# Gate and up of a SwiGLU layer as 2x2 block products in seven multiplications, on normed token halves

## The chip, the cores and the metric

The kernel runs on one core of a Trainium2 chip. Its time is the device time of one execution in microseconds (us). The engines are TensorE (PE, with its weight loads as PEld), VectorE (DVE), ScalarE (ACT), GpSimd (POOL) and SyncE (SP), whose queue issues nearly all DMAs here.

## The reference, cut to what matters

One step of a decoder layer for 1024 prompt tokens and 8 sampled tokens, 1032 rows in all, with 1024 channels. Two mixers come first (sparse attention and a gated delta rule); the change doesn't touch them. Then:

```python
x = x + jnp.sum(gates * proj, axis=2) @ w_out          # w_out [1024, 1024]
hn = rms_norm(x, norm_ffn)
gg, uu = jnp.split(hn @ w_gate_up, 2, axis=-1)         # w_gate_up [1024, 2 * 2816]
x = x + (jax.nn.silu(gg) * uu) @ w_down                # w_down [2816, 1024]
```

All of it is in float32.

## The kernel before, in words

Every large product is done on transposed data: the stationary operand is a 128x128 block of weights, the moving operand is the activations, channels on the partitions and tokens along the free axis, in three chunks of 344 tokens (`CW`, `NCH`). To keep float32 precision each operand is split exactly into a high and a low part of type float32r (`split`, L186: the high part is a copy on ACT, L187; the low part a subtraction on DVE, L188), and `mm3` (L158) forms each product from three matmuls, high-high (L163), high-low (L164) and low-high (L165). A weight slice of 128 columns comes through `split_w` (L132): one DMA to `wraw`, split to `whi` and `wlo`, two buffers of each.

The end of the kernel is `w45`. After the merge of the two mixers (`yhi`, `ylo`) comes `w_out` (L1544): for each of 8 slices and 3 chunks, 24 matmuls to a PSUM tile `pj`; its eviction adds the residual to `x2` in SBUF (L1548), squares it, splits the square, multiplies x by the gain (L1554), splits that into `hhi` and `hlo`, and lets two more matmuls with a matrix of ones add the squares of the slice to `acc` (L1557). The mean square of a token is complete only after the last slice; `rs`, its reciprocal root, is then formed on DVE (L1570 to L1576). It is not needed by the products of the feed-forward layer: `mlp` (L1585) multiplies the unnormed `hhi`, `hlo` by the weights and applies `rs` when a PSUM tile is evicted (L1604).

`mlp` has four groups of 6, 6, 5 and 5 of the 22 slices of the hidden dimension. For each slice: gate and up weights, 3 chunks of 2 x 24 matmuls, then SiLU, product and split into `act`, which stays in SBUF. After a group, its part of the down projection is added to `x2` (L1614); the last group also stores the result (`store_y`).

Order: the kernel is written as a program of tile operations, and a scheduler sets the order on each engine's queue from priorities and modelled times; at run time every engine works its queue in that order, and semaphores hold it where an operand or a buffer isn't ready. The same holds for SP's queue of DMAs.

## Time and profile before

| | us |
|---|---|
| median of 3 runs | 1839.82 |
| lowest, highest | 1836.02, 1849.74 |
| span of the profiled execution | 1845.2 |
| PE busy in it | 1797.4 (97%) |
| DVE busy, ACT busy | 1084.1 (59%), 781.3 (42%) |
| `w_out` (from 982.6 to 1083.5) | 100.9 |
| feed-forward layer to the end (from 1083.5) | 761.7 |

The profiled execution has no time of its own beside its span; that span is 5.4 us above the median of the runs. Engine times are busy times of one core. A matmul is listed with its whole duration, and matmuls overlap in the array, so the time that one takes of a stream is read from the distance of two starts, not from its duration.

### The profile page before, as it was taken

What the parts mean: (1) busy time and instruction counts of PE and PEld (TensorE: products, weight loads), DVE (VectorE), ACT (ScalarE), POOL (GpSimd) and SP (SyncE); (2) the same over time, 40 slices, a digit from 0 to 9 for tenths busy, and PEclk for the clock granted to TensorE, in tenths of its full rate; (3) what the DMA queues carried; (4) which work ended last, traced back from release to release, by engine and by line L of the source; (5) the groups of instructions that cost most, each with busy time, mean ns of one, the idle gap of its engine ahead of it and who ended that gap; (6) DMA issues with size and microseconds to landing.
All of it is one profiled execution on the core that took longest, in us unless ns stands there. A gap on an engine that the chain in (4) does not pass through costs nothing.

```text
span 1845.2 us, 29553 instructions
## 1 busy us (share of the span) xinstructions
PE 1797.4 (97%) x11532; PEld 1721.5 (93%) x11532; DVE 1084.1 (59%) x2576; ACT 781.3 (42%) x1470; POOL 42.8 (2%) x68
## 2 busy tenths in 40 slices
PE   5998999998999999999999999999999999999998
PEld 5997989998998898878799999999999999999998
DVE  7766568998898767787566573333333233333332
ACT  4567378778644345677344432211221112212222
POOL 3001100000000000000000000000000000000000
PEclk9999999999999989999999999999999999999999
DMA  6115534435456433344665111111111121021122
GB/s 190 42 37 149 158 95 120 138 114 159 109 137 180 135 108 106 133 139 161 221 204 158 38 36 50 50 44 52 48 53 38 46 58 46 29 64 35 51 62 84
DMA packets 266063, 178.82 MB, mean 97 GB/s; under 512 B 37628, under 2 KB 251456, under 8 KB 264892
## 3 DMA queue, kind: packets, MB, share of 16 engines
q1 hardware_dynamic: 264196, 166.45, 30.5%
q0 software_dynamic: 1728, 10.49, 1.6%
q8 instruction: 91, 1.49, 0.3%
q14 instruction: 48, 0.39, 0.1%
HBM read 130.98 MB, written 46.02 MB: 96 GB/s over the span
## 4 chain that ended last, share of the span: by engine, by line
PE 88%; DVE 4%; DMA 4%; ACT 2%; issue 1%; SPq 0%; DVEq 0%; ACTq 0%
PE pj L163 24%; PE pj L165 24%; PE pj L164 24%; PE PT L1054 1%; PE PT L1022 1%; PE tq L1388 1%; PE PT L1023 1%; PE PV L1058 1%; PE PV L1059 1%; PE tq L1346 1%; DMA x<-d_G 1%; DMA x<-in_x_prompt 1%; PE tp L591 1%; PE ac L410 1%; PE ac L411 1%
## 5 line engine op out<-in xcount | busy, mean ns | idle before, releaser
L163 PE MATMUL pj<-hhi,whi 128*128 128x344 f32 x1056 | 337.4, 320 | 0.1
L164 PE MATMUL pj<-hlo,whi 128*128 128x344 f32 x1056 | 336.5, 319 | 0.0
L165 PE MATMUL pj<-hhi,wlo 128*128 128x344 f32 x1056 | 334.0, 320 | 0.0
L163 PE MATMUL pj<-xhi,whi 128*128 128x344 f32 x912 | 299.1, 328 | 6.0 <-ACT gs L860 5.0
L165 PE MATMUL pj<-xhi,wlo 128*128 128x344 f32 x912 | 295.9, 324 | 0.0
L164 PE MATMUL pj<-xlo,whi 128*128 128x344 f32 x912 | 294.8, 323 | 0.0
L187 ACT ACTIVATE whi<-wraw 128x1024 fp32r<-128x1024 f32 (+2 forms) x134 | 133.3, 995 | 331.5 <-PE pj L164 328.2
L1604 DVE TENSOR_TENSOR gu<-pj,rs 128x344 f32<-128x344 f32 x132 | 68.2, 517 | 263.5 <-PE pj L165 261.4
L163 PEld LDWEIGHTS pj<-hhi,whi 128*128 128x128 f32 x1056 | 198.5, 188 | 0.4 <-DVE gu L1604 0.4
L164 PEld LDWEIGHTS pj<-hlo,whi 128*128 128x128 f32 x1056 | 198.1, 188 | 0.0
L165 PEld LDWEIGHTS pj<-hhi,wlo 128*128 128x128 f32 x1056 | 197.8, 188 | 0.0
L188 DVE TENSOR_TENSOR wlo<-wraw,whi 128x1024 fp32r<-128x1024 f32 (+2 forms) x134 | 153.1, 1142 | 50.8 <-ACT whi L187 49.3
L163 PEld LDWEIGHTS pj<-xhi,whi 128*128 128x128 f32 x912 | 173.3, 190 | 10.0 <-ACT gs L860 6.5
L164 PEld LDWEIGHTS pj<-xlo,whi 128*128 128x128 f32 x912 | 173.1, 190 | 2.0 <-issue 1.1
L165 PEld LDWEIGHTS pj<-xhi,wlo 128*128 128x128 f32 x912 | 173.1, 190 | 1.5
L164 PE MATMUL pj<-act,whi 128*128 128x344 f32 x528 | 170.2, 322 | 0.0
L163 PE MATMUL pj<-act,whi 128*128 128x344 f32 x528 | 169.7, 321 | 0.0
L165 PE MATMUL pj<-act,wlo 128*128 128x344 f32 x528 | 167.8, 319 | 0.0
L1614 DVE TENSOR_TENSOR x<-pj,x 128x344 f32<-128x344 f32 x96 | 49.6, 517 | 169.0 <-PE pj L165 169.0
L187 ACT ACTIVATE act<-gu 128x344 fp32r<-128x344 f32 x66 | 32.5, 493 | 200.4 <-DVE gu L1606 200.4
L766 DVE TENSOR_SCALAR_CACHE_REDUCE kvb<-S,cand 128x384 bf16<-128x384 f32 (+3 forms) x128 | 103.7, 810 | 2.0
L163 PEld LDWEIGHTS pj<-act,whi 128*128 128x128 f32 x528 | 99.4, 188 | 0.5
(493 smaller groups left out, 3374.2 us busy)
## 6 DMA issues: line engine op xcount, KB each, us to landing
wraw<-in_w_gate_up SPq DMA_DIRECT2D x44, 512.0 KB
wraw<-in_w_in SPq DMA_DIRECT2D x38, 512.0 KB
d_g<-gs SPq DMA_DIRECT2D x48, 172.0 KB
wraw<-in_w_branch SPq DMA_DIRECT2D x12, 512.0 KB
wraw<-in_w_down SPq DMA_DIRECT2D x16, 384.0 KB
wraw<-in_w_down SPq DMA_DIRECT2D x16, 320.0 KB
gt<-d_g SPq DMA_DIRECT2D x8, 516.0 KB
d_y<-gt SPq DMA_DIRECT2D x8, 516.0 KB
```

The lines of the kernel that those rows point to most:

```text
L163: nc.tensor.matmul(ps, lh, rh, start=(j == 0), stop=False)
L164: nc.tensor.matmul(ps, lh, rl, start=False, stop=False)
L165: nc.tensor.matmul(ps, ll, rh, start=False, stop=(j == last))
L187: self.nc.scalar.activation(hi, src, AF.Copy)
L188: self.nc.vector.tensor_tensor(lo, src, hi.bitcast(F32), op=ALU.subtract)
L410: nc.tensor.matmul(p, lhs, self.ik2[:, 0, c0:c1], start=True, stop=False)
L411: nc.tensor.matmul(p, lhs, self.ik2[:, 1, c0:c1], start=False, stop=True)
L591: nc.tensor.transpose(p[:, j, :], c[:, 128 * n:128 * n + 128], self.ident)
L766: nc.vector.tensor_scalar(junk[:r, :n], s, thr[:r, j:j + 1], 0.0, op0=ALU.is_lt, op1=ALU.add, accum_out=cnt[:r, j:j + 1])
L1022: nc.tensor.matmul(p, q2[:, j, :], self.k2[:, g, 0, a:b], start=True, stop=False)
L1604: nc.vector.tensor_tensor(s[:, e], p, rs[:, t], op=ALU.mult)
L1614: nc.vector.tensor_tensor(x2(m)[:, t], p, x2(m)[:, t], op=ALU.add)
```

## The change

The output projection and the norm are done for two halves of 516 tokens, one after the other; the normed x is written in place in `x2`, and the residual before the norm goes to DRAM (`d_x2`) to be read again before the down projection. Gate and up of one slice are seen as a 2x2 block matrix A: gate and up are its rows, the first and second 512 input channels its columns. The normed half is a 2x2 block matrix B: channel halves by two quarters of 258 tokens. The product of the two comes from seven block products, with S0 to S3 (sums and differences of blocks of A, on DVE, per slice) and T1 to T4 (differences of blocks of B, once per half). Partial products accumulate in four PSUM tags A, B, D, F with two buffers each. The first three slices (`EARLY`) are computed on half 0 in the plain way, and with seven products on half 1 alone. The hidden activations of all 22 slices go to DRAM (`d_act`), and the down projection (`down`) starts when the last slice is done and reads them back, three `araw` buffers at a time. Comments and docstrings are removed as well, which shifts the line numbers: `split` keeps L187 and L188. The removed lines stand in the section on the kernel before; the diff below leaves them out, but for a few.

```diff
-FIRST, REST = (0, 1), (2,)
+HALF, QT, EARLY = 516, 258, 3
...
+        self.d_x2 = dp.tile([8, 128, T], F32, name="d_x2")
+        self.d_act = dp.tile([22, 128, T], F32, name="d_act")
...
-        self.pj_bufs, self.tp_bufs, self.ac_bufs = 3, 2, 2
+        self.pj_bufs, self.tp_bufs = 5, 2
-        self.acc = [self.pacc() for c in range(2)]
...
     def w45(self):
...
+        H = [None, None]
+        for s in range(2):
+            self.w_out(s, (yhi, ylo), x2)
+            self.ffn_norm(s, gf, x2)
+            if s == 0:
+                H[0] = self.half_blocks(0, h0, ("B11", "B21", "B12", "B22"))
         end_y()
+        h1, end_h1 = self.pool("h1")
+        ex, end_ex = self.pool("gx")
         self.end_pf()
         self.end_ps()
+        self.ps, end_ps = self.pool("psg", space=PSUM)
+        for f in range(EARLY):
+            self.gate_up_plain(f, H[0], ex)
+        H[1] = self.half_blocks(1, h1, ("B21", "B11"))
+        H[1].update(self.half_mixes(1, h1, H[1]))
+        H[0].update(self.half_mixes(0, h0, H[0]))
+        for f in range(EARLY):
+            self.gate_up(f, (1,), H, ex)
+        for f in range(EARLY, 22):
+            self.gate_up(f, (0, 1), H, ex)
+        end_ps()
+        end_ex()
+        end_h1()
+        end_h0()
+        self.down(x2)
         end_x()
 
+    def w_out(self, s, y, x2):
+        nc, I = self.nc, self.I
+        ts = slice(HALF * s, HALF * s + HALF)
+        sq, self.sqa = self.stage[:, 0:HALF], self.stage[:, HALF * (1 + s):HALF * (2 + s)]
+        for m in range(8):
+            xv = x2(m)
+            def evac(p, t0, t1):
+                nc.vector.scalar_tensor_tensor(xv[:, t0:t1], p, 0.5, xv[:, t0:t1], op0=ALU.mult, op1=ALU.add)
+            self.proj_T(self.wcols(I['w_out'][0], 128 * m), y, evac, HALF * s, HALF * s + HALF)
+            nc.scalar.activation(sq if m else self.sqa, xv[:, ts], AF.Square)
+            if m:
+                nc.vector.tensor_tensor(self.sqa, self.sqa, sq, op=ALU.add)
+            nc.sync.dma_start(self.d_x2[m, :, ts], xv[:, ts])
+    def ffn_norm(self, s, gf, x2):
+        nc = self.nc
+        n = 86
+        p = self.pproj()
+        for j in range(6):
+            nc.tensor.matmul(p[:n, j:j + 1], self.sqa[:, n * j:n * j + n], self.ones[:, 0:1], start=True, stop=True)
+        v, r, t = (self.nrm.tile([128, 6], F32, name=x, tag=x, bufs=1)[:n] for x in ("nv", "nr", "nt"))
+        nc.vector.tensor_scalar(v, p[:n, 0:6], 1.0 / 1024, EPS, op0=ALU.mult, op1=ALU.add)
+        self.rsqrt(r, v, t=t)
+        for c in range(2):
+            p = self.pproj()
+            for j in range(3):
+                i = 3 * c + j
+                nc.tensor.matmul(p[:, n * j:n * j + n], r[:, i:i + 1].to_broadcast([n, 128]), self.ident[:n, :n],
+                                 start=True, stop=True)
+            nc.scalar.activation(self.sqa[:, QT * c:QT * c + QT], p[:, 0:QT], AF.Copy)
+        for m in range(8):
+            xv = x2(m)[:, HALF * s:HALF * s + HALF]
+            nc.vector.scalar_tensor_tensor(xv, xv, gf[:, m:m + 1], self.sqa, op0=ALU.mult, op1=ALU.mult)
+    def quarter(self, s, name):
+        i, j = int(name[1]) - 1, int(name[2]) - 1
+        t0 = HALF * s + QT * j
+        return self.x2h[i][:, :, t0:t0 + QT]
+    def block(self, pool, src):
+        t = pool.tile([128, 2, 4, QT], F32R, name="hb", tag="hb", bufs=7)
+        self.split(t[:, 0], t[:, 1], src)
+        return t
+    def half_blocks(self, s, pool, names):
+        return {x: self.block(pool, self.quarter(s, x)) for x in names}
+    def half_mixes(self, s, pool, H):
+        nc = self.nc
+        B11, B12, B21, B22 = (self.quarter(s, x) for x in ("B11", "B12", "B21", "B22"))
+        out = {}
+        def sub(name, dst, a, b):
+            nc.vector.tensor_tensor(dst, a, b, op=ALU.subtract)
+            out[name] = self.block(pool, dst)
+        if "B22" not in H:
+            out["B22"] = self.block(pool, B22)
+        sub("T1", B11, B12, B11)
+        sub("T3", B12, B22, B12)
+        sub("T2", B22, B22, B11)
+        sub("T4", B21, B21, B22)
+        return out
+    def gate_up_plain(self, f, H, ex):
+        nc, gu = self.nc, self.I['w_gate_up'][0]
+        sg = ex.tile([128, HALF], F32, name="sg", tag="sg", bufs=2)
+        ws = [self.wcols(gu, 128 * f), self.wcols(gu, 2816 + 128 * f)]
+        for e, (wh, wl) in enumerate(ws):
+            for c in range(2):
+                tag = "ABDF"[2 * e + c]
+                p = self.ps.tile([128, 512], F32, name=tag, tag=tag, bufs=2)[:, :QT]
+                x1, x2 = H[f"B1{c + 1}"], H[f"B2{c + 1}"]
+                self.mm3(p, [(wh[:, k], wl[:, k], x[:, 0, k % 4], x[:, 1, k % 4])
+                             for k in range(8) for x in ((x1, x2)[k // 4],)])
+                v = sg[:, QT * c:QT * c + QT]
+                if e == 0:
+                    nc.scalar.activation(v, p, AF.Silu)
+                else:
+                    nc.vector.tensor_tensor(v, v, p, op=ALU.mult)
+        nc.sync.dma_start(self.d_act[f, :, 0:HALF], sg)
+    def gate_up(self, f, halves, H, ex):
+        nc, gu = self.nc, self.I['w_gate_up'][0]
+        view = lambda c0: gu.rearrange("(k p) n -> p k n", p=128)[:, :, c0:c0 + 128]
+        rg, ru = (self.wp.tile([128, 8, 128], F32, name="wraw", tag="wraw", bufs=self.raw_bufs) for _ in range(2))
+        nc.sync.dma_start(rg, view(128 * f))
+        nc.sync.dma_start(ru, view(2816 + 128 * f))
+        A11, A12, A21, A22 = rg[:, 0:4], rg[:, 4:8], ru[:, 0:4], ru[:, 4:8]
+        S = [self.stage[:, 512 * j:512 * j + 512].rearrange("p (k c) -> p k c", k=4) for j in range(4)]
+        sub = lambda d, a, b: nc.vector.tensor_tensor(d, a, b, op=ALU.subtract)
+        def operand(src):
+            self.op_n = (self.op_n + 1) % 7
+            tag = ("whi", "wlo", "wx", "whi", "wlo", "wx", "wx")[self.op_n]
+            pool, bufs = (ex, 3) if tag == "wx" else (self.wp, 2)
+            t = pool.tile([128, 8, 128], F32R, name=tag, tag=tag, bufs=bufs)
+            self.split(t[:, 0:4], t[:, 4:8], src)
+            return t
+        U = {}
+        st = self.x2h[f // 2 % 2][:, 2 * (f % 2):2 * (f % 2) + 2]
+        ps = {(t, s): self.ps.tile([128, 512], F32, name=t, tag=t, bufs=2)[:, :QT] for s in halves for t in "ABDF"}
+        def product(src, x, t, first):
+            a = operand(src)
+            for s in halves:
+                b, p = H[s][x], ps[t, s]
+                for k in range(4):
+                    lh, ll, rh, rl = a[:, k], a[:, 4 + k], b[:, 0, k], b[:, 1, k]
+                    nc.tensor.matmul(p, lh, rh, start=(first and k == 0), stop=False, skip_group_check=True)
+                    nc.tensor.matmul(p, lh, rl, start=False, stop=False, skip_group_check=True)
+                    nc.tensor.matmul(p, ll, rh, start=False, stop=(k == 3), skip_group_check=True)
+        def add(e, s, c, a, b):
+            nc.vector.tensor_tensor(st[:, e, HALF * s + QT * c:HALF * s + QT * c + QT], a, b, op=ALU.add)
+        def part(tag, p=None):
+            t = ex.tile([128, QT], F32, name=tag, tag=tag, bufs=2)
+            if p is not None:
+                nc.scalar.activation(t, p, AF.Copy)
+            return t
+        product(A12, "B21", "B", True)
+        product(A11, "B11", "A", True)
+        for s in halves:
+            add(0, s, 0, part("E", ps["A", s]), ps["B", s])
+        nc.vector.tensor_tensor(S[0], A21, A22, op=ALU.add)
+        product(S[0], "T1", "D", True)
+        sub(S[1], A11, A21)
+        product(S[1], "T3", "F", True)
+        sub(S[2], S[0], A11)
+        product(S[2], "T2", "A", False)
+        for s in halves:
+            U[s] = part("U", ps["A", s])
+            e = part("E")
+            nc.vector.tensor_tensor(e, U[s], ps["D", s], op=ALU.add)
+            add(1, s, 1, e, ps["F", s])
+        sub(S[3], A12, S[2])
+        product(S[3], "B22", "D", False)
+        for s in halves:
+            add(0, s, 1, U[s], ps["D", s])
+        product(A22, "T4", "F", False)
+        for s in halves:
+            t = slice(HALF * s, HALF * s + HALF)
+            add(1, s, 0, U[s], ps["F", s])
+            nc.scalar.activation(st[:, 0, t], st[:, 0, t], AF.Silu)
+            nc.vector.tensor_tensor(st[:, 0, t], st[:, 0, t], st[:, 1, t], op=ALU.mult)
+            nc.sync.dma_start(self.d_act[f, :, t], st[:, 0, t])
+    op_n = -1
+    def down(self, x2):
+        nc, dn = self.nc, self.I['w_down'][0]
+        self.pf, self.end_pf = self.pool("psd", space=PSUM)
+        self.pj_bufs = 4
+        self.open_psum("ps6")
+        ac, end_ac = self.pool("act", side="right")
         wk, end_wk = self.pool("mlp")
+        for m in range(8):
+            nc.sync.dma_start(x2(m), self.d_x2[m])
         groups = [(0, 6), (6, 12), (12, 17), (17, 22)]
         for gi, (f0, f1) in enumerate(groups):
+            act = []
             for f in range(f0, f1):
+                a = ac.tile([128, 2, T], F32R, name="act", tag="act", bufs=10)
+                raw = wk.tile([128, T], F32, name="araw", tag="araw", bufs=3)
+                nc.sync.dma_start(raw, self.d_act[f])
+                self.split(a[:, 0], a[:, 1], raw)
+                act.append((a[:, 0], a[:, 1]))
             for m in range(8):
+                def evac(p, t0, t1):
+                    xv = x2(m)[:, t0:t1]
+                    nc.vector.tensor_tensor(xv, p, xv, op=ALU.add)
+                self.proj_T(self.wcols(dn[128 * f0:128 * f1], 128 * m, f1 - f0), act, evac)
                 if gi == len(groups) - 1:
                     self.store_y(m, x2, wk)
         end_wk()
         end_ac()
+        self.end_ps()
+        self.end_pf()
 
...
```

How the order on the queues changes, at three places.

**PE, end of the output projection.** Before: the products of the next stage (`hhi`) stand right behind those of `w_out` (`yhi`), and the sums of squares (`ac`, L1557) among them.

```order
L163 MATMUL pj<-yhi,whi 128x344
L164 MATMUL pj<-ylo,whi 128x344
L165 MATMUL pj<-yhi,wlo 128x344
L163 MATMUL pj<-hhi,whi 128x344
L164 MATMUL pj<-hlo,whi 128x344
L165 MATMUL pj<-hhi,wlo 128x344
...
L1557 MATMUL ac<-sqh,onesr 128x344
```

Now, at the end of half 0 (`rs` in the first row is the sum of squares, `nr` the reciprocal roots; the rows with `whi_11333` are the last slice of half 0, those with `whi_11445` the first of half 1):

```order
L164 MATMUL pj_11364<-ylo_10251,whi_11333 128x258
L165 MATMUL pj_11364<-yhi_10250,wlo_11334 128x258
L1589 MATMUL pj_11393<-ones_1543,rs_10113 86x1 x6
L1597 MATMUL pj_11414<-ident_84,nr_11401 128x86 x3
L1597 MATMUL pj_11419<-ident_84,nr_11401 128x86 x3
L163 MATMUL pj_11450<-yhi_10250,whi_11445 128x258
L164 MATMUL pj_11450<-ylo_10251,whi_11445 128x258
```

The twelve small matmuls of the norm stand between two streams with nothing else between them; at the end of half 1 it is the same, with the first plain gate slice behind them.

**DVE, one slice of gate and up.** Before (`gu` is a pair of evicted tiles):

```order
L1604 TENSOR_TENSOR gu_14208<-pj_14235,rs_10113 128x344
L1606 TENSOR_TENSOR gu_14208<-gu_14208 128x344
L188 TENSOR_TENSOR wlo_14274<-wraw_14272,whi_14273 128x1024
L188 TENSOR_TENSOR act_14081<-gu_14208,act_14081 128x344
L1604 TENSOR_TENSOR gu_14278<-pj_14279,rs_10113 128x344
L1604 TENSOR_TENSOR gu_14278<-pj_14305,rs_10113 128x344
```

Now, from the split of A22 of slice 4 to the first addition after the fifth product of slice 4 (`wraw_13229` and `wraw_13230` are gate and up weights of slice 5, of which S0 to S3 are formed; names with 13003 to 13008 are PSUM tiles of slice 4):

```order
L188 TENSOR_TENSOR wx_13194<-wraw_12999,wx_13194 128x512
L188 TENSOR_TENSOR whi_13241<-wraw_13229,whi_13241 128x512
L1688 TENSOR_TENSOR x20_10114<-E_13064,B_13003 128x258
L1688 TENSOR_TENSOR x20_10114<-E_13067,B_13007 128x258
L188 TENSOR_TENSOR wlo_13268<-wraw_13229,wlo_13268 128x512
L1699 TENSOR_TENSOR rs_10113<-wraw_13230 128x512
L1663 TENSOR_TENSOR rs_10113<-wraw_13229,wraw_13230 128x512
L1663 TENSOR_TENSOR rs_10113<-rs_10113,wraw_13229 128x512
L188 TENSOR_TENSOR wx_13302<-rs_10113,wx_13302 128x512
L1663 TENSOR_TENSOR rs_10113<-wraw_13229,rs_10113 128x512
L188 TENSOR_TENSOR whi_13330<-rs_10113,whi_13330 128x512
L1708 TENSOR_TENSOR E_13156<-U_13154,D_13004 128x258
```

The operands of a slice are made about two thirds of a slice ahead, and the addition L1708, on whose result PE's next product into D waits, stands behind S0 (L1699), which needs the up weights of the slice after it.

**SP, from gate and up to the down projection.** Before, only weights follow each other here:

```order
L139 DMA wraw<-in_w_gate_up 128x8x128 x10
L139 DMA wraw<-in_w_down 128x5x128 x8
```

Now (the first row is the output of the last slice on half 0, the third that on half 1; `d_x` is `d_x2`):

```order
L1720 DMA d_act<-x_10114 128x516
L1739 DMA araw<-d_act 128x1032 x3
L1720 DMA d_act<-x_10114 128x516
L1732 DMA x_10114<-d_x_108 128x1032
L1739 DMA araw<-d_act 128x1032
L1732 DMA x_10114<-d_x_108 128x1032
L1739 DMA araw<-d_act 128x1032 x7
```

No activations are read back before the last slice's half 0 is done, and from the fourth on each read waits for one of the three `araw` buffers.

## Rows read from the trace of the kernel before

**Rows 1.** The head of every view: core and span.

```profile
core 0 of [0], span 1845.2 us
```

**Rows 2.** Windows, output projection and feed-forward: busy us by engine, PEclk, DMA share, GB/s.

```profile
982.60:1083.50 100.90, 100.34 (x642) 99.49 (x641) 55.88 (x110) 40.91 (x86) 0.00 (x0) 1.00 0.20 60
1095.00:1776.00 681.00, 680.91 (x4332) 680.63 (x4331) 248.28 (x415) 127.96 (x199) 0.00 (x0) 1.00 0.16 46
```

**Rows 3.** Groups by line and shape: gate and up, output projection, sums of squares.

```profile
L163 PE MATMUL pj<-hhi,whi 128*128 128x344 f32 x1056 | 337.4, 320 | 0.1
L163 PE MATMUL pj<-yhi,whi 128*128 128x344 f32 x192 | 61.5, 320 | 0.0
L1557 PE MATMUL ac<-sqh,onesr 128*128 128x344 f32 x32 | 10.2, 326 | 0.0
L1557 PE MATMUL ssa<-sqh,onesr 128*128 128x344 f32 x16 | 5.1, 319 | 0.0
```

**Rows 4.** Timeline, TensorE, 344 columns: start us, duration us, instruction.

```profile
1773.83 0.32 PE L165 MATMUL pj<-hhi,wlo 128*128 128x344 f32 x1
...
1776.97 0.32 PE L165 MATMUL pj<-act,wlo 128*128 128x344 f32 x1
```

**Rows 5.** Timeline, TensorE, 256 columns, two stretches.

```profile
858.72 0.27 PE L1023 MATMUL PT<-k,q 128*128 128x256 f32 x1
...
859.07 0.60 PE L1054 MATMUL PT<-ident,P 128*128 128x128 f32 x4
...
868.85 0.28 PE L1023 MATMUL PT<-k,q 128*128 128x256 f32 x1
...
869.21 0.60 PE L1054 MATMUL PT<-ident,P 128*128 128x128 f32 x4
```

**Rows 6.** Timeline, TensorE, 128 columns.

```profile
885.94 0.27 PE L1023 MATMUL PT<-k,q 128*128 128x128 f32 x1
...
886.50 0.37 PE L163 MATMUL pj<-o,whi 128*128 128x344 f32 x1
```

**Rows 7.** Timeline, ScalarE, end of the output projection (in brackets: idle before, releaser).

```profile
1083.66 1.06 ACT L187 ACTIVATE whi<-wraw 128x1024 fp32r<-128x1024 f32 x1 [2.09 <-PE pj L164]
```

**Rows 8.** Timeline, VectorE, end of the output projection.

```profile
1085.11 1.21 DVE L188 TENSOR_TENSOR wlo<-wraw,whi 128x1024 fp32r<-128x1024 f32 x1
1086.24 0.33 DVE L1572 TENSOR_SCALAR rs<-hnt 128x344 int32<-128x344 int32 x1
1086.49 0.51 DVE L188 TENSOR_TENSOR hlo<-hnt,hhi 128x344 fp32r<-128x344 f32 x1
1086.91 0.51 DVE L188 TENSOR_TENSOR sqh<-sq,sqh 128x344 fp32r<-128x344 f32 x1
```

**Rows 9.** Timeline, VectorE, a reciprocal root on four columns, step by step.

```profile
641.92 0.17 DVE L196 TENSOR_SCALAR oss<-oss 128x4 int32<-128x4 int32 x1
...
643.70 0.16 DVE L200 SCALAR_TENSOR_TENSOR oss<-rst,oss 128x4 f32<-128x4 f32 x1
```

**Rows 10.** Timeline, TensorE, sixteen small float32 matmuls in a row.

```profile
654.05 1.95 PE L1464 MATMUL tq<-skq,st 128*128 128x2 f32 x16
```

**Rows 11.** Windows, TensorE alone: busy us (matmuls), granted clock, DMA share, GB/s.

```profile
907.00:910.00 3.00, 0.95 (x4) 0.94 0.43 176
910.00:917.00 7.00, 7.00 (x34) 0.54 0.96 331
917.00:924.00 7.00, 7.00 (x63) 1.00 0.90 308
```

**Rows 12.** Timeline, SyncE's queue: two weight loads issued.

```profile
969.29 0.37 SPq L154 DMA_DIRECT2D wraw<-in_w_branch  x1
...
972.97 0.38 SPq L139 DMA_DIRECT2D wraw<-in_w_out  x1
```

**Rows 13.** Timeline, ScalarE: the splits that waited for these two loads.

```profile
974.30 1.06 ACT L187 ACTIVATE whi<-wraw 128x1024 fp32r<-128x1024 f32 x1 [1.53 <-DMA wraw<-in_w_branch]
...
979.26 1.06 ACT L187 ACTIVATE whi<-wraw 128x1024 fp32r<-128x1024 f32 x1 [1.36 <-DMA wraw<-in_w_out]
```

70 lines of the change are left out of this document (2 added, 68 removed).

## The prediction

> **What bounds the kernel now.** I read the windows first. In the 681 us of gate, up and most of down TensorE is busy 680.9 us at the full clock, VectorE 248 us, ScalarE 128 us, and the DMA engines a sixth [rows 2]. The output projection ahead is as full [rows 2]. So nothing but TensorE sets the time from 982.6 us to the end, and a change pays there by what it takes from TensorE's stream, less the holes that it opens. The groups give the counts: the row of hhi stands for one of three alike, so gate and up are 3 x 1056 = 3168 matmuls of 344 columns, the output projection 3 x 192 = 576, the sums of squares 32 + 16 = 48 [rows 3]. The reader should see in the timeline that the duration shown, 320 ns, is not the price: from the first to the last of 21 starts in a row it is 3.14 us, 157 ns each [rows 4]. Gate and up then cost 3168 x 0.157 = 497.4 us.
>
> **Matmuls of gate and up.** A slice with seven products has 7 x 4 x 3 x 2 = 168 matmuls of 258 columns, a plain half 2 x 2 x 8 x 3 = 96, half a slice with seven products 84. That is 19 x 168 + 3 x (96 + 84) = 3732. The columns fall by 12%, the number of matmuls rises by 18%, so the price of one at 258 columns decides. No row has 258. At 256 columns, three steps take 0.35 us and three others 0.36 us, 118 ns each [rows 5]; at 128 columns, where half of that would do, five steps still take 0.56 us, 112 ns each [rows 6], so there is a floor, and 258 lies just above it. I take 119 ns, from the nearest row: 3732 x 0.119 = 444.1 us, a gain of **53.3 us**. The ends are the floor, 112 ns (gain 79.4), and 157 ns, if a matmul cost the same whatever its columns (loss 88.5).
>
> Each of these matmuls loads its own weights, and the stream shows that the load lies beside other matmuls: 157 ns for 344 columns is less than a load of about 112 (the floor) and a stream of 157 one after the other would take [rows 4, 6]. [...]
>
> **Output projection.** 768 matmuls of 258 columns in place of 576 of 344: 91.4 against 90.4 us, **+1.0**. The sums of squares on TensorE go: 48 x 0.157, **-7.5**. The weights are loaded and split twice; with VectorE busy 56 of 101 us there [rows 2] and less per eviction than before, I cost that at nothing; without cover it would be 8 splits of 1.1 us.
>
> **The two norms.** Before, the reciprocal root was wanted only at evictions, and TensorE went on. Now the small matmuls of the norm stand right behind a half's last product in TensorE's order, and the next stream right behind them. From the last product: drain and residual add, 0.6 us; on ScalarE the high part of the next weights stands ahead of the last square, 1.06 us [rows 7], then the square, 0.6 (estimate), done at 1.8; on VectorE the low part of those weights, 1.13 us (step from 1085.11 to 1086.24 [rows 8]), ends at 2.4, the sum of squares at 3.0; six small float32 matmuls at 0.11 us each (1.95 us for 16 less one 0.3 long [rows 10]) and their drain, 4.0; eleven tiny VectorE steps at 0.2 us (nine steps from 641.92 to 643.70 [rows 9]), 6.2; six more small matmuls, 7.0. Twice 7.0 is **+14.0**. Bounds: 5 each if the weight split is out of the way, 9 if each hand-over costs more.
>
> **The clock after a hole.** [...] That is 7 x (1 - 34/63) = 3.2 us lost. Each hole of 7 us should bring the same, and the one below: 3 x 3.2, **+9.7**. Bounds 0 and 15.
>
> **The start of down.** The reads of the stored activations stand on SP behind the store of the last slice's half 0, which comes some 1.5 us before TensorE is done. Three reads go out at about -1.1 us. Two loads of 512 KB took from issue to use 974.30 - 969.29 = 5.0 us and 979.26 - 972.97 = 6.3 us [rows 12, 13]; with 5.0 the first lands at 3.9, its split ends at 6.2 (1.06 and 1.13 us). The fourth read waits for that split, lands at 11.3, is split at 13.6; the fifth and sixth follow at 15.4 and 16.7. TensorE works slice by slice, 12 x 0.157 = 1.9 us on each, and ends the sixth near 18.0, having done 11.3 us of work: **+7**. Bounds 4 (landing in 4 us) and 10 (6.3 us). The residual's 4.2 MB are read before, on idle DMA engines: nothing.
>
> **VectorE and ScalarE.** Steps are 0.43 us for 344 columns (1086.49 to 1086.91) and 1.13 for 1024 [rows 8], so 0.34 for 258, 0.60 for 512, 0.61 for 516, 1.14 for 1032 (estimates on that line). A slice: 7 low parts and 4 sums of 0.60, 10 additions of 0.34, 2 products of 0.61, 11.2 us of VectorE against 168 x 0.119 = 20.0 of TensorE: hidden. Beside the three plain slices stand the gain of half 1 (8 x 0.61), eight block low parts (8 x 1.14), four mixes (4 x 1.14), six weight low parts (6 x 1.14) and six products (6 x 0.34), 27 us, beside 288 x 0.119 = 34 us of TensorE; a half slice needs 8.9 us beside 10.0. That is tight and ordered in one queue: **+2**, between 0 and 6. If that cover fails, the blocks of half 1 are late, and TensorE waits at the first half slice.
>
> **Sum.** -53.3 + 1.0 - 7.5 + 14.0 + 9.7 + 7 + 2 = -27.1 us. Against the profiled execution's 1845.2 us [rows 1] it gives 1818; that execution is 5.4 us above the median, so against 1839.8 I predict **1813 us**. Everything ahead of the merge keeps its order and costs the same.
>
> **Rivals.** *Cheap holes* (0.15): the holes are 5 us, the clock doesn't follow, a matmul is at 117 ns: -60.8 + 1 - 7.5 + 10 + 0 + 4 = -53, 1787. For: the floor allows it. Against: 34 matmuls against 63.
>
> *Small waits in every slice* (0.18, no change): TensorE's second product into D waits for an addition that stands behind S0 in VectorE's queue, and buffers turn over once a slice. At 1 us in each of 19 slices it is -27 + 19 = -8, 1832. For: one queue order, many partners. Against: my chain leaves 2 us.
>
> *Late up weights* (0.10, slower): the same place, another cause. A slice's up weights can be loaded only when the slice before has split its A22, near 0.9 us after the start of its product A11; from landing, three sums, two splits, one more sum and the addition take 4.2 us, and the addition must be done 112 matmuls, 13.3 us, after that start. So it decides from a landing of 8.2 us. At 10.6 us each slice waits 2.4: -27 + 46 = +19, 1859. Against: 5.0 and 6.3 us, at DMA shares well above the 0.16 of this stage [rows 2].
>
> *Weight loads show* (0.07, slower): every matmul loads new weights, and in a long stream at 258 columns they may not hide. Break-even is (497.4 - 26.2) / 3732 = 126 ns; at 140 ns, midway between the 256- and the 344-column row, the loss is 51 us, 1891. Against: the 118 ns of rows 5, each with its own load. The full form, every load in series with its stream, makes the loss 10 + 26 = 36 us, 1876, and has 0.01 of the 0.07. [...]
>
> That the change computes less than it says is excluded by the order, which lists the 3732 matmuls.
>
> **Numbers.** The forecast, 1795 to 1830, has 0.50. This kernel's runs tell 1% (18 us) from no change. Faster by more than that is below 1821: 0.15 and 0.43 of the forecast, 0.58. Within 1%: the forecast's other 0.07 and 0.18, 0.25. Slower: 0.10 and 0.07, 0.17. The range, 1785 to 1846, leaves out the two slower rivals and 0.02 at the far end of the cheap one; the likeliest case's own range is 1795 to 1830.
>
> **What would show it.** In the profile after: starts 119 ns apart in a slice; two holes of 7 us around the norms, and a slice distance near 20.0 us; a granted clock near 0.5 behind each hole; ScalarE's splits of araw waiting for DMAs at the start of down, TensorE late by 7 us. I am wrong if slices lie over 21 us apart, if starts lie 126 ns or more apart, or if the holes are filled.

## The result and the profile after

| | before | changed |
|---|---|---|
| median, us | 1840.86 (4 runs) | 1817.86 (4 runs) |
| lowest, highest | 1836.02, 1849.74 | 1812.77, 1822.79 |
| span of the profiled execution | 1845.2 | 1820.4 |

The ratio is 0.9874, with a 95% interval of 0.9833 to 0.9914: 23 us faster, where 27 were forecast, and 1817.9 us where 1813 were. In a second set of runs the same kernel had 1818.32 against 1837.93 us, 0.9888 (0.9851 to 0.9925).

One thing has to be settled before two profiles are compared. The part of the program ahead of the output projection, which the change leaves alone, doesn't take the same time in every execution: the first matmul of the output projection starts at 982.7 us before, at 978.8 after, and between 967.9 and 986.6 us in the eleven profiles of changed kernels (this one and the ten below). That spread is as large as the gain. So from here on stages are counted from that matmul, called the start. From the start to the end of the span it was 862.5 us and is 841.6 us, **20.9 us less**; the second profile of the changed kernel has 843.1, 19.4 less.

The windows of the profile after show the stages (busy time of each engine and number of its instructions, granted clock, DMA share):

```profile
core 0: us, PE busy (x) PEld busy (x) DVE busy (x) ACT busy (x) POOL busy (x), PEclk, DMA share, GB/s
978.80:1029.00 50.20, 48.66 (x407) 48.23 (x404) 23.80 (x39) 16.47 (x24) 0.00 (x0) 1.00 0.51 161
1029.00:1040.00 11.00, 5.88 (x33) 5.68 (x32) 4.78 (x16) 2.35 (x4) 0.00 (x0) 0.65 0.23 72
...
1086.30:1098.00 11.70, 6.58 (x39) 6.29 (x38) 5.85 (x17) 3.64 (x5) 0.00 (x0) 0.67 0.21 68
...
1165.00:1546.00 381.00, 381.00 (x3170) 381.00 (x3170) 237.60 (x436) 130.67 (x246) 0.00 (x0) 1.00 0.29 89
1547.00:1554.00 7.00, 3.01 (x11) 2.61 (x11) 2.36 (x3) 1.29 (x2) 0.00 (x0) 0.79 0.91 289
1554.00:1561.00 7.00, 6.25 (x35) 5.33 (x34) 3.70 (x3) 2.97 (x3) 0.00 (x0) 0.96 0.95 350
```

Beside [rows 2] the reader sees two stretches that weren't there: in 1029 to 1040 and in 1086.3 to 1098 us TensorE is busy half the time. Between them and behind them it is full, and in the 381 us of steady slices it does 3170 matmuls, 120 ns each. The last two windows are the start of down: 11 and 35 matmuls where a full 7 us hold 44.

The price of a matmul is read from starts, as in [rows 4]. The last products of gate and up, and the first of down, in the timeline of TensorE (start, duration, then instruction; in brackets the idle time ahead and what ended it):

```profile
1542.75 0.28 PE L1682 MATMUL F<-hb,wx 128*128 128x258 f32 x1
1542.87 0.28 PE L1683 MATMUL F<-hb,wx 128*128 128x258 f32 x1
...
1546.95 0.28 PE L1684 MATMUL F<-hb,wx 128*128 128x258 f32 x1
1551.22 1.51 PE L163 MATMUL pj<-act,whi 128*128 128x344 f32 x4 [3.99 <-ACT act L187]
```

From 1542.75 to 1546.95 there are 36 starts, 120 ns apart. Over 40 us of a steady stretch (1300 to 1340 us, 333 starts) it is 120.3 ns; before, over the same 40 us (254 starts), 157.2. The numbers in the windows are a little higher than starts, since an instruction that reaches over an edge counts on both sides. Then comes a hole: the first matmul of down waits 3.99 us for ScalarE's split of the first activation slice.

### The profile page after: what moved, and what is told of

Read it like the earlier page. It is cut to its first block, busy times and chain, and to the rows that moved or that the text cites. A ratio compares the mean times of both kernels' runs of the same rounds, so it can differ in the third digit from the quotient of the medians.

```text
span 1820.4 us, 31736 instructions
## 1 busy us (share of the span) xinstructions
PE 1754.0 (96%) x12288; PEld 1676.4 (92%) x12288; DVE 1212.4 (67%) x2776; ACT 852.5 (47%) x1575; POOL 42.6 (2%) x68
## 4 chain that ended last, share of the span: by engine, by line
PE 83%; DMA 6%; DVE 5%; issue 3%; ACT 2%; SPq 0%; POOL 0%; ACTq 0%; DVEq 0%; POOLq 0%
PE pj L163 15%; PE pj L164 15%; PE pj L165 15%; PE D L1682 2%; PE D L1683 2%; PE F L1682 2%; PE F L1684 2%; PE D L1684 2%; PE F L1683 2%; PE A L1684 2%; PE A L1682 2%; PE A L1683 2%; PE PT L1055 1%; DMA wraw<-in_w_gate_up 1%; PE B L1682 1%
## 5 line engine op out<-in xcount | busy, mean ns | idle before, releaser
L187 ACT ACTIVATE whi<-wraw 128x1024 fp32r<-128x1024 f32 (+3 forms) x126 | 115.2, 914 | 253.1 <-PE pj L164 220.8
L188 DVE TENSOR_TENSOR wlo<-wraw,whi 128x1024 fp32r<-128x1024 f32 (+2 forms) x104 | 116.4, 1119 | 47.7 <-ACT whi L187 45.8
L163 PEld LDWEIGHTS pj<-act,whi 128*128 128x128 f32 x528 | 99.1, 189 | 6.4 <-ACT act L187 5.0
L164 PEld LDWEIGHTS pj<-act,whi 128*128 128x128 f32 x528 | 99.7, 189 | 2.2 <-DVE act L188 2.2
L165 PEld LDWEIGHTS pj<-act,wlo 128*128 128x128 f32 x528 | 99.7, 189 | 0.0
L1682 PE MATMUL D<-hb,wx 128*128 128x258 f32 x328 | 93.1, 284 | 0.0
L1683 PE MATMUL D<-hb,wx 128*128 128x258 f32 x328 | 92.9, 283 | 0.0
L1683 PE MATMUL A<-hb,wlo 128*128 128x258 f32 x328 | 92.8, 283 | 0.0
L1684 PE MATMUL A<-hb,wlo 128*128 128x258 f32 x328 | 92.8, 283 | 0.0
L1682 PE MATMUL A<-hb,wlo 128*128 128x258 f32 x328 | 92.7, 283 | 0.0
L1684 PE MATMUL D<-hb,wx 128*128 128x258 f32 x328 | 92.6, 282 | 0.0
```

The lines of the kernel that those rows point to most:

```text
L163: nc.tensor.matmul(ps, lh, rh, start=(j == 0), stop=False)
L164: nc.tensor.matmul(ps, lh, rl, start=False, stop=False)
L165: nc.tensor.matmul(ps, ll, rh, start=False, stop=(j == last))
L187: self.nc.scalar.activation(hi, src, AF.Copy)
L188: self.nc.vector.tensor_tensor(lo, src, hi.bitcast(F32), op=ALU.subtract)
L1682: nc.tensor.matmul(p, lh, rh, start=(first and k == 0), stop=False, skip_group_check=True)
```

## The experiments

Each is an edit of the changed kernel. Where an expectation gives 11.2 us as TensorE's loss at the start of down, it counts the transposes at the end too cheaply; counted directly (321 matmuls in the 60 us behind the last product, where 380 fit at 157.5 ns) the loss is 9.3 us. All losses below are counted in this way, and differences between kernels don't hang on it.

**Plain products on all slices.**

```diff
-        for f in range(EARLY, 22):
-            self.gate_up(f, (0, 1), H, ex)
+        for f in range(EARLY, 22):
+            self.gate_up_plain(f, (0, 1), H, ex)
```

(The first three slices, and the blocks of half 1, likewise.)

> Gate and up of all 22 slices in the plain way on both halves; everything else as in the changed kernel (halves, norms ahead of the products, activations through DRAM). Theory A (the gain is the smaller number of matmuls at a price that goes by columns): 22 x 2 x 96 = 4224 matmuls of 258 columns at the 120.4 ns that the changed kernel shows are 508.6 us against 449.3, so TensorE's gate and up take 59 us longer than in the changed kernel and the time is about 1877 us, some 36 us above the kernel before. Theory B (the gain comes from what else the change moves, for instance the norm that left the evictions, and not from the number of matmuls): the time stays within 10 us of the changed kernel's 1818. In A the two norm holes (9.6 and 9.0 us) and the late start of down stay as they are.

Measured: from the start to the end 893.1 us, 51.5 more than the changed kernel, 30.6 more than before; one run, 1862.75 us beside 1836.59 before. (That it lies 14 us under the 1877 of theory A is for the most part the early start of this execution, 967.9 us against 978.8.) Gate and up alone take 508.4 us from first to last product: with 1.8 us for the fallen clock taken off, 4224 matmuls at 119.9 ns. The price is the same as with seven products within half a nanosecond, only their number differs. Theory A holds; of its 59 us, 57 show in gate and up (508.4 against 451.6), and 3.4 come back at the start of down, where this kernel loses 5.9 us. So the halves, the norm ahead and the way through DRAM, with 8 us for products of 258 columns in place of 344 (4224 times 119.9 ns against 3168 times 157.2), are a cost by themselves, and only the smaller number of matmuls pays for them.

**Matmuls that nobody reads in the norm holes.**

```diff
+        self.idle(20)                       # 20 products of yhi with itself
         p = self.pproj()
         for j in range(6):
             nc.tensor.matmul(p[:n, j:j + 1], self.sqa[...], self.ones[:, 0:1], ...)
...
         self.rsqrt(r, v, t=t)
+        self.idle(15)
```

> The changed kernel with extra matmuls whose result nobody reads in each norm hole: 20 between the last product and the first six small ones, 15 between these and the second six (2.4 and 1.8 us, inside the 2.9 and 2.2 us in which TensorE sat idle). Theory A (the price of the clock is paid after the hole and goes back to TensorE's idle time in it): the holes keep their 9.6 and 9.0 us, but the matmuls behind them start 0.12 us apart from the first on, instead of 0.215 us for 16 to 24 of them; 2 x 2 us less, and the small matmuls of the second batch (2.86 us for 12 records) shrink too, towards 1.5 us: 5 to 7 us less in all. Theory B (the granted clock falls whatever TensorE does with so few matmuls): starts 0.215 us apart as before, no gain. Theory C (the extra matmuls delay the chain): holes of 10 to 13 us, 2 to 6 us more.

First the hole as it is in the changed kernel, half 0, in the timeline of TensorE:

```profile
1028.85 0.28 PE L165 MATMUL pj<-yhi,wlo 128*128 128x258 f32 x1
1032.02 1.71 PE L1589 MATMUL pj<-ones,rs 128*86 128x1 f32 x12 [2.90 <-DVE rs L1580]
1035.95 2.86 PE L1597 MATMUL pj<-ident,nr 86*128 86x86 f32 x12 [2.22 <-DVE nr L200]
1038.53 0.56 PE L163 MATMUL pj<-yhi,whi 128*128 128x258 f32 x1
1038.89 0.42 PE L164 MATMUL pj<-ylo,whi 128*128 128x258 f32 x1
```

The same hole on VectorE: the addition of the residual, the low part of the next weights, the sum of squares, then the first and the last of eleven small steps.

```profile
1029.16 0.43 DVE L1576 SCALAR_TENSOR_TENSOR x<-pj,x 128x258 f32<-128x258 f32 x1 [2.45 <-PE pj L165]
1030.13 1.22 DVE L188 TENSOR_TENSOR wlo<-wraw,whi 128x1024 fp32r<-128x1024 f32 x1 [0.55 <-ACT whi L187]
1031.28 0.69 DVE L1580 TENSOR_TENSOR rs<-rs 128x516 f32<-128x516 f32 x1
1033.77 0.16 DVE L1591 TENSOR_SCALAR nv<-pj 86x6 f32<-86x6 f32 x1 [1.80 <-PE pj L1589]
...
1035.73 0.16 DVE L200 SCALAR_TENSOR_TENSOR nr<-nt,nr 86x6 f32<-86x6 f32 x1
```

And TensorE at the same place with the extra matmuls (L1611):

```profile
1018.97 2.54 PE L1611 MATMUL pj<-yhi 128*128 128x258 f32 x20
1022.03 1.08 PE L1591 MATMUL pj<-ones,rs 128*86 128x1 f32 x12 [0.52 <-DVE rs L1581]
1022.97 2.03 PE L1611 MATMUL pj<-yhi 128*128 128x258 f32 x15
1025.33 1.57 PE L1600 MATMUL pj<-ident,nr 86*128 86x86 f32 x12 [0.33 <-DVE nr L200]
1026.69 0.37 PE L163 MATMUL pj<-yhi,whi 128*128 128x258 f32 x1
1026.89 0.28 PE L164 MATMUL pj<-ylo,whi 128*128 128x258 f32 x1
```

The six small matmuls stand as twelve records. With TensorE idle ahead of them, the second batch takes 2.6 us (1035.95 to 1038.53), and the products behind it start 0.21 us apart, twice the 0.12; the granted clock in 1035 to 1042 us is 0.50. With the extra matmuls the second batch takes 1.4 us (1025.33 to 1026.69) and the products start 0.12 us apart at once. The hole shrinks from 9.6 to 7.7 us in half 0 and from 9.0 to 7.7 in half 1. From the start to the end it is 835.4 us, 6.2 less (one run, 1805.91 us). Theory A; its "the holes keep their 9.6 and 9.0 us" was too cautious, since the small matmuls inside the hole run at the lower clock too (the second batch 2.6 us against 1.4).

**The norm between other products.**

```diff
-        for s in range(2):
-            self.w_out(s, (yhi, ylo), x2)
-            self.ffn_norm(s, gf, x2)
+        self.w_out(0, (yhi, ylo), x2, range(8))
+        norm = self.ffn_norm(0, gf, x2, self.pproj)
+        self.w_out(1, (yhi, ylo), x2, range(1))
+        next(norm)                          # sums, reciprocal root
+        self.w_out(1, (yhi, ylo), x2, range(1, 2))
+        next(norm, None)                    # its broadcast, gains
...
+            for _ in self.gate_up_plain(f, H[0], ex):
+                next(norm, None)            # half 1: behind gate, behind up
```

> The changed kernel with other products of TensorE between the steps of each norm: for half 0 the first two weight slices of the output projection of half 1, for half 1 the gate and the up part of the first plain slice; 48 matmuls, 5.8 us, stand ahead of each batch of six small ones. Theory A (the holes are only a matter of order, and the clock falls because of them): both holes close (9.6 and 9.0 us), no stretch near half clock behind them (2 x 2 us), 21 to 23 us less than the changed kernel, near 1796 us. Theory B (the work is only put off: gains, blocks and mixes of half 1 come later on VectorE, and TensorE waits for them at the first half slice): 10 to 15 us less, with waits of 5 to 10 us for splits near the first half slice. Theory C (the small steps on VectorE now stand behind evictions, and TensorE waits for the reciprocal root as long as before): less than 8 us gained.

Measured: 1803.37 us (1798.10 to 1811.66, 4 runs), ratio to before 0.9823 (0.9780 to 0.9867); from the start to the end 829.6 us, 12.0 less than the changed kernel. Both holes are gone, and yet only half of the 21 to 23 us of theory A came. From the start to the last product 555.5 us are left of 568.2. The small matmuls are TensorE's own work and don't vanish (2.3 us a norm in the kernel with the extra matmuls: 1022.03 to 1022.97 and 1025.33 to 1026.69), and what follows is later. The windows around the first half slices:

```profile
core 0: us, PE busy (x) PEld busy (x) DVE busy (x) ACT busy (x) POOL busy (x), PEclk, DMA share, GB/s
1099.00:1106.00 7.00, 7.00 (x61) 7.00 (x60) 6.82 (x9) 5.11 (x8) 0.00 (x0) 1.00 0.27 77
1106.00:1113.00 7.00, 6.97 (x58) 6.76 (x56) 7.00 (x12) 3.01 (x5) 0.00 (x0) 1.00 0.11 39
1113.00:1120.00 7.00, 4.89 (x27) 4.68 (x28) 4.98 (x9) 2.69 (x5) 0.00 (x0) 0.76 0.52 150
1120.00:1127.00 7.00, 7.00 (x60) 7.00 (x60) 6.78 (x12) 3.90 (x7) 0.00 (x0) 1.00 0.33 99
1127.00:1134.00 7.00, 6.50 (x52) 6.08 (x51) 4.66 (x9) 3.24 (x7) 0.00 (x0) 1.00 0.32 91
```

TensorE's waits there, in sum (engine, tile and line that waited, what it waited for, us, times, longest):

```profile
PE A L1693 <- DVE wlo L188: 1.2, 1, 1.2
PE D L1691 <- DVE E L1717: 0.9, 1, 0.9
PE B L1691 <- ACT whi L187: 0.5, 1, 0.5
```

VectorE is busy for 7.0 of 7 us, TensorE waits for its splits and additions, and in 1113 to 1120 us the clock falls to 0.76. Against 61 in a full window the 58, 27, 60 and 52 are some 5 us at 120.3 ns each. In the changed kernel the norm hole had given VectorE that time. That is theory B, at 12 us.

**Six buffers at the start of down.**

```diff
-        for m in range(8):
-            nc.sync.dma_start(x2(m), self.d_x2[m])
...
-                raw = wk.tile([128, T], F32, name="araw", tag="araw", bufs=3)
+                raw = wk.tile([128, T], F32, name="araw", tag="araw", bufs=6)
...
+            if gi == 0:
+                for m in range(8):
+                    nc.sync.dma_start(x2(m), self.d_x2[m])
```

> The changed kernel with six buffers for the activations read back instead of three, and the reads of the residual that are still open at that point issued behind the first six of them. TensorE loses 11.2 us at the start of down in the changed kernel. Theory A (the loss is a chain of latencies: three reads, then a read that waits for a split to free its buffer): reads four to six are issued at once behind the first three, the sixth split ends some 5 us earlier, and TensorE loses 6 to 7 us; 4 to 5 us less. Theory B (the DMA engines, 0.84 to 0.96 busy from 1546 to 1560 us, are the limit): the six reads share the same rate and land when they did, no more than 1 us less. In both the first matmul comes 4 us after the last product, since the first read isn't issued earlier.

**Two slices read back early.**

```diff
+        self.early = [ea.tile([128, T], F32, name="ea", tag="ea", bufs=2) for f in range(2)]
+        for f in range(2):
+            nc.sync.dma_start(self.early[f], self.d_act[f])
         self.gate_up(21, (0, 1), H, ex)
```

(With it, five buffers in place of three, and the residual's reads behind the first group's.)

> The changed kernel with the first two activation slices read back before the last gate and up slice, into two buffers of their own, five buffers for the others, and the residual's open reads behind the first group's. From the last product to the last down matmul less the 254.9 us of work in between, TensorE lost 11.2 us in the changed kernel, 8.0 with six buffers alone. Theory A (what is left with six buffers is the landing of the first read, 4 us after its issue, and the split behind it): with two slices there before the last product, the first split follows the last SiLU at once, TensorE starts some 1.5 us after the last product instead of 4.1, its clock doesn't fall, and it loses 4 to 5 us. Theory B (the rate of the DMA engines decides): the third slice lands when it did, TensorE waits there instead, and loses 7 to 8 us.

ScalarE's splits of the first six slices, in the timeline of the changed kernel:

```profile
1550.11 1.06 ACT L187 ACTIVATE act<-araw 128x1032 fp32r<-128x1032 f32 x1 [3.18 <-DMA araw<-d_act]
1553.77 1.06 ACT L187 ACTIVATE act<-araw 128x1032 fp32r<-128x1032 f32 x1 [2.60 <-DMA araw<-d_act]
1555.07 1.07 ACT L187 ACTIVATE act<-araw 128x1032 fp32r<-128x1032 f32 x1 [0.24 <-DMA araw<-d_act]
1558.27 1.07 ACT L187 ACTIVATE act<-araw 128x1032 fp32r<-128x1032 f32 x1 [2.13 <-DMA araw<-d_act]
1561.33 1.06 ACT L187 ACTIVATE act<-araw 128x1032 fp32r<-128x1032 f32 x1 [2.00 <-DMA araw<-d_act]
1562.60 1.07 ACT L187 ACTIVATE act<-araw 128x1032 fp32r<-128x1032 f32 x1 [0.20 <-DMA araw<-d_act]
```

And the issues of their reads on SP's queue there (start, time on the queue, count):

```profile
1546.05 2.02 SPq L1739 DMA_DIRECT2D araw<-d_act  x3
...
1552.47 0.32 SPq L1739 DMA_DIRECT2D araw<-d_act  x1
...
1556.16 11.42 SPq L1739 DMA_DIRECT2D araw<-d_act  x6
```

The first three reads go out together at 1546.05 and are split from 1550.11 on; the fourth is issued at 1552.47, when the first split has freed its buffer, and is split at 1558.27; the next go out from 1556.16. With six buffers the six splits begin at 1540.34, 1542.46, 1544.27, 1546.17, 1548.31 and 1549.59 us, so the sixth lies 9.3 us behind the first instead of 12.5. TensorE's loss falls from 9.3 to 6.2 us, and from the start to the end it is 837.8 us, 3.8 less (one run, 1808.74 us): nearer to theory A than to B. The run changes two things at once, the buffers and the place of the residual's reads; what each is worth by itself isn't shown. With two slices there in time:

```profile
1556.36 2.00 ACT L187 ACTIVATE act<-ea 128x1032 fp32r<-128x1032 f32 x2
1559.74 1.07 ACT L187 ACTIVATE act<-araw 128x1032 fp32r<-128x1032 f32 x1 [1.38 <-DMA araw<-d_act]
1561.40 1.06 ACT L187 ACTIVATE act<-araw 128x1032 fp32r<-128x1032 f32 x1 [0.58 <-DMA araw<-d_act]
```

The first split begins before the last product is done, TensorE starts 0.9 us behind it, and loses 4.0 us in all; from the start to the end 838.1 us, 3.5 less than the changed kernel. Of the 5.3 us that the start of down gains, the stages ahead of it take some back: from the start to the last product it is 569.9 us, against 568.2 and 569.6 in the two profiles of the changed kernel. (The one run's 1826.4 us contain the latest start of all, 986.6.) What is left is the third slice, read behind the last stores, and the clock, 0.79 in the 7 us behind the last product.

**The changed kernel again.**

> The changed kernel unchanged, on the same chip as the three others of this set, since the part of the program ahead of the output projection differed by up to 14 us between the profiles so far (first matmul of the output projection at 967.9 to 982.7 us). Theory A (that part varies by execution, not by kernel): the output projection starts between 967 and 983 us here too, and from there to the end it takes the 841.6 us of the first profile within 4 us. Theory B (the change itself moved that part): the start lies near 978.8 again while the other kernels of the set, which share the change, differ from it by their edits alone.

The start lies at 973.1 us, between those of kernels that share this part of the program (969.0 to 986.6 in this set), and from there to the end it takes 843.1 us against 841.6. Theory A: the part ahead varies by itself, and the stages behind it agree within 1.5 us. The kernel before has one profile, so whether the change also moves the part ahead by a few microseconds isn't shown.

**All mends, and a fourth plain slice.**

```diff
+        p = self.ps.tile([128, 512], F32, name="F", tag="F", bufs=2)[:, :128]
+        for j in range(28):
+            nc.tensor.matmul(p, z, z, start=(j == 0), stop=(j == 28 - 1))
```

(Behind the last slice's products, with the edits on the norm and on early reads.) The other kernel of the pair adds:

```diff
-HALF, QT, EARLY = 516, 258, 3
+HALF, QT, EARLY = 516, 258, 4
```

> All mends together: the norm's steps between other products, two slices read back early and five buffers, and 28 matmuls of 128 columns that nobody reads behind the last gate and up product, so that TensorE isn't idle while the first split runs. From the first matmul of the output projection to the end the changed kernel took 841.6 us, with the filled holes 829.6. Theory A (the mends add up): 5 to 7 us less at the start of down, 822 to 825 us, some 17 to 19 us under the changed kernel run beside it. Theory B (the start of down is set by the rate of the DMA engines): 827 to 829 us.

> The same with four plain slices on half 0 ahead of the seven-product slices instead of three. With the filled holes alone TensorE lost 3.9 us to waits and a fall of the clock between 1106 and 1148 us, where VectorE was busy 7.0 of 7 us. Theory A (VectorE is the limit there, and needs more time ahead): 12 matmuls more, 1.4 us, and the 3.9 us of waits gone: 2 to 2.5 us less than with three. Theory B (each half slice waits by itself, for its own additions and splits, however many plain slices stand ahead): the waits stay, one half slice more, 1.4 to 2.5 us more than with three.

| | median, us (6 runs) | ratio to before | start to end | loss at down |
|---|---|---|---|---|
| all mends | 1796.47 | 0.9776 (0.9744 to 0.9809) | 824.0 | 3.2 |
| and four plain slices | 1796.14 | 0.9775 (0.9745 to 0.9805) | 822.5 | 3.2 |

The mends add up (theory A: 822 to 825): 21.9 us under the changed kernel's 1818.32 in the same set, 41 under the kernel before. The fourth plain slice is no gain that the runs can tell. The waits for VectorE at the first half slice are gone, as its theory A says, but a wait for ScalarE's part of the weights comes up in 1141 to 1148 us, where TensorE does 39 matmuls, and with 1.4 us for the matmuls added it takes most of the gain back.

**Chunks of 172 columns in down.**

```diff
-                self.proj_T(self.wcols(dn[...], 128 * m, f1 - f0), act, evac)
+                w = self.wcols(dn[...], 128 * m, f1 - f0)
+                for q in range(6):
+                    self.proj_T(w, act, evac, 172 * q, 172 * q + 172)
```

First in the changed kernel, then in the one with all mends.

> The changed kernel with the down projection in six chunks of 172 tokens instead of three of 344: 3168 matmuls instead of 1584, the same columns in all. It shows how far the price of a matmul goes on falling with its columns below 258. Theory A (there is a floor near the 112 ns that the 128-column matmuls of the kernel before show, set by what comes with each matmul and not by its columns): 3168 x 0.112 = 355 us against 1584 x 0.158 = 250, so 105 us more, near 1920 us. Theory B (the price is 0.46 ns a column, as between 258 and 344 columns, and the 112 ns at 128 columns came from those few matmuls alone): 79 ns, 250 us, no change beyond what the evictions add. In between, a start distance of 90 to 100 ns would say that part of the load hides.

> The kernel with all mends (no idle stretch of TensorE at the start of down), with the down projection in six chunks of 172 tokens. With six chunks in the changed kernel the granted clock fell in the hole at the start of down and stayed at 0.50 from 1554 to 2097 us although TensorE was busy all the time: matmuls 214 ns apart; behind 2104 us, at 1.00, they lie 107 ns apart. Theory A (the clock fell because of the hole, and this stream can't bring it back): without the hole the granted clock stays at 1.00, 3168 x 0.107 = 339 us against 250, and the time is near 1796 + 89 = 1885 us. Theory B (the stream of 172 columns lets the clock fall by itself): 0.50 here too, 3168 x 0.214 = 678 us less what runs at full clock at the end, and the time is near 2160 us.

The windows of down, in the changed kernel with chunks of 172:

```profile
core 0: us, PE busy (x) PEld busy (x) DVE busy (x) ACT busy (x) POOL busy (x), PEclk, DMA share, GB/s
1540.00:1547.00 7.00, 6.51 (x55) 6.30 (x53) 4.68 (x10) 1.66 (x3) 0.00 (x0) 1.00 0.37 102
1547.00:1554.00 7.00, 2.64 (x12) 2.30 (x12) 1.93 (x2) 1.87 (x2) 0.00 (x0) 0.83 0.95 301
1554.00:1561.00 7.00, 6.63 (x30) 6.13 (x29) 3.70 (x3) 2.38 (x3) 0.00 (x0) 0.50 0.87 298
1600.00:1700.00 100.00, 100.00 (x471) 100.00 (x471) 13.57 (x31) 4.23 (x5) 0.00 (x0) 0.50 0.07 20
...
2090.00:2097.00 7.00, 7.00 (x35) 7.00 (x35) 0.67 (x2) 0.04 (x1) 0.00 (x0) 0.50 0.00 0
2097.00:2104.00 7.00, 7.00 (x48) 7.00 (x48) 1.84 (x4) 2.16 (x4) 0.00 (x0) 0.71 0.40 120
```

and in the kernel without the hole:

```profile
core 0: us, PE busy (x) PEld busy (x) DVE busy (x) ACT busy (x) POOL busy (x), PEclk, DMA share, GB/s
1525.00:1532.00 7.00, 7.00 (x64) 7.00 (x62) 4.96 (x7) 2.97 (x4) 0.00 (x0) 1.00 0.81 227
...
1600.00:1700.00 100.00, 100.00 (x898) 100.00 (x897) 30.93 (x64) 12.62 (x14) 0.00 (x0) 1.00 0.20 64
1700.00:1800.00 100.00, 100.00 (x898) 100.00 (x897) 34.01 (x73) 13.35 (x16) 0.00 (x0) 1.00 0.13 39
```

The first takes 2184.23 us, the second 1900.29 (one run each). Neither theory of the first run foresaw it: the clock falls in the hole at the start of down (0.83 in 1547 to 1554 us), and then TensorE stays at a granted clock of 0.50 from 1554 to 2097 us, from 1571 us on without a gap, with 471 matmuls in 100 us, 213 ns each. Without the hole the granted clock is 1.00 from 1525 to 1546 and from 1600 to 1880 us, and a matmul takes 111.7 ns (896 starts from 1600 to 1700 us). That is theory A of the second run; its 1885 us took 107 ns, and with 111.7 the same sum gives 1900. The price at full clock settles the first question: 111.7 ns for 172 columns and 112 for 128 [rows 6], so there is a floor, and 258 columns with 120.3 stand just above it.

## Why the forecast came out

| step | forecast, us | measured |
|---|---|---|
| gate and up: matmuls | -53.3 | -49.0 |
| output projection | +1.0 | +1.9 |
| sums of squares | -7.5 | -7.5 |
| norm holes, two | +14.0 | +15.4 at full clock |
| clock in and behind them | +6.4 | +7.2 |
| start of down, with its clock | +10.2 | +9.3 |
| VectorE and ScalarE | +2 | 0 |
| not foreseen (below) | 0 | +1.8 |
| sum | -27.1 | -20.9 |

The forecast's 9.7 us for three falls of the clock stand here as 6.4 and 3.2, the latter with the start of down; rounding leaves 0.1 in the sum. The first three measured rows are numbers of matmuls times distances of starts. All measured terms together make the 20.9 us from the start to the end.

**Matmuls.** The count was right and the price of before too (157.2 for 157). After, it is 120.3 ns, not 119; 3732 times 1.3 ns is 4.9 us, the largest miss of the sum. The choice of the nearest row [rows 5] was right as a choice, but three steps read to 0.01 us can't tell 118 ns from 120. Behind the floor the curve climbs, from 111.7 at 172 over 120.3 at 258 to 157.2 at 344. A load in series with its stream, the full form of *weight loads* among the rivals, is shown by no run: at the forecast's own prices it would be 112 + 157 = 269 ns before and 112 + 119 = 231 ns after, from which its 10 us of loss come (3732 times 231 ns against 3168 times 269). The runs show 157.2 and 120.3 ns in place of these, with a weight load to each matmul: from 1165 to 1546 us 3170 of each, and both busy for all 381.00 us. That the floor is the time of a load was the forecast's estimate; the runs show how high the floor is, not what makes it.

**Norm holes.** On VectorE the chain came as forecast: the sum of squares is done 3.0 us behind the last product (1031.97 less 1028.97), the low part of the weights stands ahead of it, and the small steps take 2.1 us. What failed is the two batches of small matmuls: 1.0 and 0.8 us in the forecast, 1.7 and 2.6 in half 0, 1.2 and 2.6 in half 1. They come after idle time, and all but the first of half 1 and the beginning of the first of half 0 ran at the lower clock (0.81 in 1028 to 1035 us, 0.50 in 1035 to 1042 and in 1091 to 1098); the forecast put the clock's price only behind the hole, at 3.2 us each by the counts of [rows 11] (7 us at a granted clock of 0.54, 34 matmuls against 63), of which 1.7 and 2.3 us were found there. With the clock kept up, the hole was 7.7 us, for a forecast of 7.0. Hole and clock together were sized right, 20.4 against 22.6, with the parts at other places.

**Start of down.** The chain of waits was named as it came: the reads behind the last slice's first store, a landing of some 4 us, the fourth read behind the first split. From the last product's end (1547.07), the fourth slice's landing was forecast at 11.3 us and came at 11.2 (1558.27). That it fits so well is in part luck: the first read took 4.1 us from issue to split where 5.0 were taken, the fourth 5.8. The end of the sixth split was forecast at 16.7 us and came at 17.9 (1564.93), TensorE's end of the sixth slice near 18.0 and came at 19.9 (1566.99). The loss is 9.3 us for 10.2, clock included. The experiments show two parts of it, the buffers with the residual's reads moved behind them (3.1 us) and the first landing (2.2 more). "Nothing" for the residual's reads was perhaps not quite right: some of them are still open then, with the DMA engines 0.91 and 0.95 busy; what they cost wasn't tried by itself.

**VectorE.** No wait of TensorE over 0.3 us between the first and the last product of gate and up: the profile after lists only those in the norm holes and at down. The cover held because the norm hole had given VectorE time, as the filled holes show by taking it away.

**Not foreseen.** Transposes of x still stand ahead of the first products and hold TensorE once for 1.5 us, 1.1 us more than before; the end behind the last product of down takes 0.7 us more. Their causes weren't tried.

Of the rivals, *cheap holes* fell with the 9.6 and 9.0 us, *small waits in every slice* with a distance of slices of 20.2 us (168 times 120.3 ns, and the stores of two slices at 1508.57 and 1528.77 us), *late up weights* and *weight loads* with the same row. The forecast was right in its mechanism; gains and losses were each sized within 5 us, and the errors, mostly against the gain, put it 6 us off from the start to the end, and 5 us off the median.

## What to carry to other kernels

Here fewer, shorter matmuls paid by columns only down to the floor: 258 columns keep nearly all of the gain (0.466 ns a column against 0.457 at 344), while at 172 columns a matmul costs 111.7 ns, 0.65 a column. An estimate from these: another halving of the columns would sit on the floor and lose the gain; it wasn't tried. A step that needed a whole result before the next product could start cost the chain, holes of 9.6 and 9.0 us, and the clock behind it, 1.7 and 2.3 us more; other products placed between its pieces closed both holes and brought back only 12.0 us of the 21 to 23 expected, since VectorE, which feeds the products, was then busy for 7.00 of 7 us. So the engine that feeds them needs the time. Where nothing else is at hand there are matmuls that nobody reads: here they kept the products behind the norm 0.12 us apart in place of 0.21, 6.2 us less from the start to the end. And where the stage ahead varies by more than the effect, count from a common instruction.

## What the runs showed of the hardware

A busy TensorE didn't come back to full clock at once in these runs. With 258 columns the products behind a norm hole ran at a granted clock of 0.50 for some 4 to 5 us (0.21 us apart from 1038.53 to 1042.54 and from 1095.46 to 1100.55); with 172 columns for 543 us, the last 526 of them without a gap, until the last group's transposes came in (48 instructions in 2097 to 2104 us, 65 in the next 7), while the same stream without the hole was at 1.00 from 1600 to 1880 us. The two runs lie 284 us apart, of which 22 are the other mends; the 2553 matmuls at half clock, at 213.3 ns in place of 111.7, account for the other 260. So the few microseconds of holes at the start of down cost some 260 us in this run. Each of the two ran once, so whether every execution of the first stays at 0.50 isn't shown. In its stretch from 1600 to 1700 us TensorE was busy for 100.00 of 100 us at a granted clock of 0.50. What in the last group brought it back wasn't tried.

The small matmuls of the norm (one column of 128x86, and 86x86, in plain float32) each stand as two records, 0.08 and 0.11 us from start to start with the extra matmuls ahead of them, against 0.15 and 0.21 in the hole of half 0 of the changed kernel, at granted clocks of 0.81 (1028 to 1035 us) and 0.50 (1035 to 1042 us).
